# Transposing V in fp32 through a shared ring of PSUM banks in a cross-covariance attention kernel

## The chip, the cores and the metric

The kernel runs on one core of one Trainium2 chip. The metric is the device time of one execution in microseconds (us). Beside the times there is one execution recorded by the hardware profiler, from which all views come.

The engines are named as in the profile: PE is TensorE (matrix multiplies and transposes), PEld its weight loads, DVE is VectorE, ACT is ScalarE, POOL is GpSimd, and SP is SyncE, which issues every transfer of this kernel. SPq is SP's own instruction queue. SBUF is the core's working memory. PSUM is the memory that PE writes its results into; it has eight banks of 2 KB for each of the 128 partitions.

## What is computed

```python
def setup_inputs():
    batch, heads, seq, dim = 8, 12, 512, 64      # Q, K, V: float32
...
    Q_norm = Q / (np.linalg.norm(Q, axis=-2, keepdims=True) + 1e-10)
    K_norm = K / (np.linalg.norm(K, axis=-2, keepdims=True) + 1e-10)
    attn = np.einsum('bhnd,bhne->bhde', Q_norm, K_norm)
    attn = np.exp(attn - np.max(attn, axis=-1, keepdims=True))
    attn = attn / (np.sum(attn, axis=-1, keepdims=True) + 1e-10)
    return np.einsum('bhnd,bhde->bhne', V, attn).astype(np.float32)
```

There are 96 heads. For each, Q and K give a 64 x 64 matrix, which is normalised by the column norms, put through a softmax along its rows, and then multiplied from the left by V. Three inputs and one output of 12.6 MB each make 50.3 MB of transfers.

## The kernel before

Four heads make a unit, and there are 24 units (`U`). One transfer brings Q, K or V of a unit as a tile of 128 partitions x 1024 fp32 (512 KB): each head takes 32 partitions (`NV`), each holding 16 rows (`R`) of 64 values.

Per unit the work is this. `cast_q` and `cast_k` (VectorE) round Q and K into one bf16 tile `qkb`. `grams` (L94) multiplies it by its own transpose, 64 small matmuls, so that one 128 x 128 result per head holds K'Q as well as the squared norms on its diagonal; it goes to `gbuf`, which takes four PSUM banks and exists once. `norms` (L106) takes the diagonals out on VectorE, and GpSimd raises them to the power -1/2 (`rq`, L111). `keep_kq` (L99, ScalarE) copies the K'Q part out of `gbuf`, `scale_k` (L116, GpSimd) scales it, `logits` (L122) transposes it on PE in fp32, `scale_q` (L126) scales it again, `exps` (L130) takes the exponential and `normalise` divides by the row sums. The result is a bf16 matrix in `abuf`; `doubled` (L152) puts a copy of it onto the other 64 partitions, by a matmul and a copy on ScalarE.

V needs a transpose, as its rows must become columns for the last multiply. `cast_v` (L87) rounds it to bf16 into `vb`. `vtrans` (L144) transposes eight 128 x 128 blocks on PE into the bank `vps`, and ScalarE copies the whole bank to SBUF as `vt` (L147), interleaving two blocks on the way. `outs` (L163) multiplies, in two halves of eight matmuls, each half into one bank `po`, and copies each half into `so` (L167). `store` sends `so` out.

PSUM is split so: four banks for `gbuf`, one for the logits and the doubled matrix (`lg` and `dup`), one for `vps`, two for `po`.

The order is written out by hand. The main loop runs over `s`, one step for each unit of Q and K, and is pipelined by hand: step `s` casts unit s + 1, makes the grams and norms of s, the logits of s - 1, and the normalised matrix of s - 2. V and outputs lag behind by the rule `outs_by`, four units in five steps, so that of five steps four have one V and one output. Every engine executes its own instructions in the order written. SP issues the loads three units ahead, and stores three units late, in one queue; at most eight transfers are under way.

When the main loop ends, 16 units have their outputs. The tail does the other eight: `gbuf`'s four banks are freed for transposes (`ps_t`), VectorE takes over the casts of V, and the two copies of an output are split between ScalarE and VectorE (`both`).

Of the kernel before, what the change touches and what calls it, by code (L numbers as in the profile page):

```python
# [8 lines left out]
F32 = mybir.dt.float32  # L9
BF16 = mybir.dt.bfloat16  # L10
# [4 lines left out]
D = 64  # L15
HU = 4
NV = 32
R = 16
SV = 2
MV = 64  # L20
TP = 4
# [3 lines left out]
def kernel(  # L25
# [7 lines left out]
    nc = tc.nc  # L33
    B, H, N, _ = Q.shape
    assert N == NV * R and Q.shape[3] == D
    U = B * H // HU
# [5 lines left out]

    const = ctx.enter_context(tc.tile_pool(name="const", bufs=1))
    qp = ctx.enter_context(tc.tile_pool(name="qp", bufs=5))
    vp = ctx.enter_context(tc.tile_pool(name="vp", bufs=6))
    vbp = ctx.enter_context(tc.tile_pool(name="vbp", bufs=4))
    qkp = ctx.enter_context(tc.tile_pool(name="qkp", bufs=4))
    vtp = ctx.enter_context(tc.tile_pool(name="vtp", bufs=3))
    sop = ctx.enter_context(tc.tile_pool(name="sop", bufs=10))
    small = ctx.enter_context(tc.tile_pool(name="small", bufs=4))  # L50
    main = ctx.enter_context(ExitStack())
    ps_v = ctx.enter_context(tc.tile_pool(name="ps_v", bufs=1, space=bass.MemoryType.PSUM))
    ps_l = ctx.enter_context(tc.tile_pool(name="ps_l", bufs=1, space=bass.MemoryType.PSUM))
    ps_o = ctx.enter_context(tc.tile_pool(name="ps_o", bufs=2, space=bass.MemoryType.PSUM))

    LOAD_AHEAD = 3

    def outs_by(s):

        return max(0, (s - 2) * 4 // 5)  # L60


    qf, kf, vf, vb, qkb, nsq, rq, kqs, sl, ex, vt, so, kq = ({} for _ in range(13))

    def load_qk(u):
        qf[u] = qp.tile([128, R, D], F32, name="qf")
# [4 lines left out]
    def load_v(u):  # L71
        vf[u] = vp.tile([128, R * D], F32, name="vf")
        nc.sync.dma_start(out=vf[u], in_=Vf[u])

    def store(u, g=slice(0, SV)):
        nc.sync.dma_start(out=Of[u][:, g], in_=so[u][:, g].rearrange("p s t d -> p s (t d)"))
# [4 lines left out]

    def cast_k(u):
        nc.vector.tensor_copy(qkb[u][:, :, D:], kf[u])  # L83

    def cast_v(u, copy=nc.scalar.copy):
        w = vb[u] = vbp.tile([128, R // 2, 2 * D], BF16, name="vb")
        copy(w.rearrange("p t d -> p (t d)"), vf[u])  # L87

    def grams(u):

# [29 lines left out]
    def logits(u):  # L120
        for h in range(HU):
            nc.tensor.transpose(lg[:, h, :], kqs[u][D:, h, :], ident[D:, D:])  # L122

    def scale_q(u):
        s = sl[u] = small.tile([D, HU, D], F32, name="sl")
        nc.vector.tensor_tensor(out=s, in0=lg, in1=rq[u][0:D, :, None].to_broadcast([D, HU, D]), op=ALU.mult)  # L126

    def exps(u):
        e = ex[u] = small.tile([D, HU, D], F32, name="ex")
        nc.scalar.activation(e, sl[u], AF.Exp)  # L130

    def normalise(u):
        s = small.tile([D, HU], F32, name="esum")
        nc.vector.reduce_sum(out=s, in_=ex[u], axis=AX.X)  # L134
        ri = small.tile([D, HU], F32, name="rinv")
        nc.vector.reciprocal(ri, s)
        a = abuf[u % len(abuf)]
        nc.vector.tensor_tensor(out=a[0:D, :, 0, :], in0=ex[u], in1=ri[:, :, None].to_broadcast([D, HU, D]), op=ALU.mult)  # L138

    def vtrans(u, pool=ps_v):  # L140

        ps = pool.tile([128, R // 2, 128], BF16, name="vps")
        for t in range(R // 2):
            nc.tensor.transpose(ps[:, t, :], vb[u][:, t, :], identb)  # L144

        w = vt[u] = vtp.tile([128, TP, 128, 2], BF16, name="vt")
        nc.scalar.copy(w.rearrange("p t c a -> p a t c"), ps.rearrange("p (a t) c -> p a t c", a=2))  # L147

    def doubled(u):

        a = abuf[u % len(abuf)]
        nc.tensor.matmul(dup[D:], identb[0:D, 0:D], a[0:D, :, 0, :], tile_position=(0, D))  # L152
        nc.scalar.copy(a[D:, :, 1, :], dup[D:])  # L153

    def outs(u, copies=(nc.scalar.copy, nc.scalar.copy)):
        s = so[u] = sop.tile([128, SV, TP, 2 * D], F32, name="so")
        a = abuf[u % len(abuf)]
        for g in range(SV):
            po = ps_o.tile([128, TP, 2 * D], F32, name="po")
            for t in range(TP):  # L160
                for x in range(2):
                    h = 2 * g + x
                    nc.tensor.matmul(  # L163
                        po[MV * x:MV * (x + 1), t, :], vt[u][:, t, NV * h:NV * (h + 1), :].rearrange("p c a -> p (c a)"),
                        a[:, h].rearrange("p a d -> p (a d)"), tile_position=(0, MV * x),
                    )
            copies[g](s[:, g], po)  # L167

    ps_g = main.enter_context(tc.tile_pool(name="ps_g", bufs=1, space=bass.MemoryType.PSUM))
    gbuf = ps_g.tile([128, HU, 512], F32, name="gram")  # L170
# [8 lines left out]
    ident = const.tile([128, 128], F32, name="ident")  # L179
    make_identity(nc, ident)  # L180
    identb = const.tile([128, 128], BF16, name="identb")
# [4 lines left out]
    for i in range(12):  # L186
        a = const.tile([128, HU, 2, D], BF16, name=f"ab{i}")
# [3 lines left out]
    def on(f, u):  # L191
        if 0 <= u < U:
            f(u)
# [5 lines left out]
    nv, nst, nt = 2, 0, 0  # L199
    for s in range(U):  # L200
        n0, n1 = outs_by(s - 1), outs_by(s)
        on(load_qk, s + LOAD_AHEAD)
        while nv < min(U, n1 + 4):
            load_v(nv)
            nv += 1
        while nst < n1 - 3:
            store(nst)
            nst += 1
        new = range(nt, n1 + 1) if s >= 1 else ()
        for v in new:  # L210
            cast_v(v)
        on(cast_q, s + 1)
        on(normalise, s - 2)
        on(grams, s)
        on(norms, s)
        on(keep_kq, s)
        on(scale_k, s)
        on(logits, s - 1)
        on(scale_q, s - 1)
        on(exps, s - 1)  # L220
        on(cast_k, s + 1)
        for v in range(n0, n1):
            outs(v)
        on(doubled, s - 2)
        for v in new:
            vtrans(v)
            nt = v + 1

    last = U - 1
    main.close()  # L230
    ps_t = ctx.enter_context(tc.tile_pool(name="ps_t", bufs=4, space=bass.MemoryType.PSUM))
    both = (nc.scalar.copy, nc.vector.tensor_copy)

    def v_ahead(u):
        if u + 1 < U:
            vtrans(u + 1, ps_t)

    def cast_ahead(u):
        if u < U:
            cast_v(u, nc.vector.tensor_copy)  # L240

    def move(u):
        on(load_v, u + 4)
        store(u - 3)

    cast_ahead(n1 + 1)
    cast_ahead(n1 + 2)
    for i, u in enumerate(range(n1, U)):
        move(u)
        v_ahead(u)  # L250
        if i == 0:
            normalise(last - 1)
        if i == 1:
            logits(last)
            scale_q(last)
            exps(last)
        if i == 2:
            normalise(last)
        if i >= 1:
            cast_ahead(u + 2)  # L260
        outs(u, both)
        if i == 0:
            doubled(last - 1)
        if i == 2:
            doubled(last)
# [34 lines left out]
```

## Time and profile before

| | |
|---|---|
| median of 3 runs | 134.99 us (133.66 to 135.82) |
| the profiled execution | 131.46 us, span of the core 129.7 us |
| transfers | 50.34 MB in 97 of 512 KB or less, all issued by SP |
| rows of V: cast on ScalarE, L87 | 17, 1046 ns each |
| cast on VectorE, L87 | 7, 679 ns each |
| copy of vt, L147 | 24, 1311 ns each |
| copies of so, L167 | 40 on ScalarE, 593 ns; 8 on VectorE, 688 ns |
| last gram | ends at 108.0 us |
| last copy into so | starts at 125.3 us |

A row of a group in the profile reads: line, engine, operation, result <- inputs with their shapes, how often; then busy time and mean ns of one; then how long the engine sat idle just before these instructions, and on whom it waited. In the view of waits, a row says who waited for whom, the sum in us, the number of times and the longest. "Granted clock" is the share of full speed at which PE runs; in this profile it is either 1.0 or 0.5 at any moment. A clock of 1.0 is also what the view prints ahead of the first record, which comes after some 43 us here; in the first 31 us the 64 gram matmuls take 1.89 us as they do at half clock later, against 1.07 us at full clock.

### The profile page before, as it was taken

How to read it: one execution, taken by the hardware profiler on the slowest of the kernel's cores; microseconds unless marked ns; L12 is line 12 of the kernel's file. 1: busy time of each engine (PE TensorE's matmuls, PEld its weight loads, DVE VectorE, ACT ScalarE, POOL GpSimd, SP SyncE). 2: the span in 40 equal slices, each digit the busy share in tenths (PEclk: the TensorE clock that was granted, in tenths of full speed). 3: DMA queues.
4: the chain of work that ended last, by engine and by line, in shares of the span. 5: the costliest groups of instructions: out<-in, count | busy, mean ns of one | idle time of the engine just before them, and what ended most of it. 6: DMA issues, size and time to landing. Idle time of an engine off the chain costs nothing.

```text
span 129.7 us, 5416 instructions
## 1 busy us (share of the span) xinstructions
PE 90.5 (70%) x2232; PEld 69.5 (54%) x2232; DVE 94.7 (73%) x351; ACT 96.8 (75%) x154; POOL 71.0 (55%) x68
## 2 busy tenths in 40 slices
PE   0034878699677789859866996567999774968630
PEld 0043666568455668638543874455768553745520
DVE  0776687985987788785988498698956968588640
ACT  3002442658999958999995879999779999889960
POOL 7924467773873578383778368187717773500000
PEclk9999999999999555995896579998555999599996
DMA  4999999999999999999999999999999999989885
GB/s 140 394 417 418 412 401 411 408 402 407 409 402 412 412 409 408 414 407 411 407 418 406 416 409 416 410 415 413 410 416 408 409 403 419 407 336 361 324 318 214
DMA packets 16936, 50.67 MB, mean 391 GB/s; under 512 B 1552, under 2 KB 1552, under 8 KB 16912
## 3 DMA queue, kind: packets, MB, share of 16 engines
q1 hardware_dynamic: 16912, 50.34, 97.9%
q8 instruction: 17, 0.28, 0.8%
q14 instruction: 7, 0.06, 0.1%
HBM read 37.75 MB, written 12.58 MB: 388 GB/s over the span
## 4 chain that ended last, share of the span: by engine, by line
ACT 32%; PE 26%; DMA 14%; DVE 9%; POOL 8%; issue 7%; SPq 1%; ACTq 0%; POOLq 0%; DVEq 0%
DMA qf<-in_Q_dram 14%; ACT vt L147 12%; ACT so L167 8%; PE gram L94 8%; PE po L163 7%; PE vps L144 6%; POOL rq L111 6%; ACT vb L87 3%; PE lgdup L122 3%; ACT kq L99 3%; DVE scr L106 3%; ACT ab L153 3%; ACT ex L130 2%; PE lgdup L152 2%; POOL kqs L116 2%
## 5 line engine op out<-in xcount | busy, mean ns | idle before, releaser
L111 POOL TENSOR_TENSOR rq<-nsq,mhalf 128x4 f32<-128x4 f32 x24 | 49.3, 2056 | 38.2 <-DVE nsq L106 23.1
L94 PE MATMUL gram<-qkb 32*128 32x128 bf16 x1536 | 37.3, 264 | 15.5 <-DVE qkb L83 11.6
L94 PEld LDWEIGHTS <-qkb 32*128 32x128 bf16 x1536 | 31.2, 119 | 24.3 <-DVE qkb L83 17.8
L106 DVE CUSTOM_DVE_ANT_0 scr<-gram,ident 128x128 f32<-128x128 f32 x96 | 22.1, 284 | 16.2 <-PE gram L94 16.2
L147 ACT COPY vt<-vps 128x1024 bf16<-128x1024 bf16 x24 | 31.5, 1311 | 1.6 <-PE vps L144 1.0
L99 ACT COPY kq<-gram 64x256 f32<-64x256 f32 x24 | 8.8, 367 | 23.2 <-DVE nsq L106 22.9
L80 DVE CAST qkb<-qf 128x1024 bf16<-128x1024 f32 x24 | 19.3, 803 | 5.0 <-DMA qf<-in_Q_dram 4.9
L167 ACT COPY so<-po 128x512 f32<-128x512 f32 x40 | 22.1, 593 | 0.9 <-PE po L163 0.5
L163 PE MATMUL po<-ab,vt 128*64 128x128 bf16 x384 | 19.2, 251 | 4.6 <-ACT so L167 2.2
L144 PE MATMUL vps<-identb,vb 128*128 128x128 bf16 x192 | 18.2, 250 | 1.5 <-DVE vb L87 1.3
L163 PEld LDWEIGHTS <-vt 128*64 128x64 bf16 x384 | 14.5, 128 | 8.5 <-ACT vt L147 4.6
L87 ACT CAST vb<-vf 128x1024 bf16<-128x1024 f32 x17 | 17.8, 1046 | 0.7 <-DMA vf<-in_V_dram 0.6
L144 PEld LDWEIGHTS <-vb 128*128 128x128 bf16 x192 | 13.2, 111 | 8.2 <-DVE vb L87 3.2
L122 PE MATMUL lgdup<-ident,kqs 64*64 64x64 f32 x96 | 12.6, 269 | 7.1 <-POOL kqs L116 6.6
L116 POOL TENSOR_TENSOR kqs<-kq,rq 64x256 f32<-64x256 f32 x24 | 15.1, 628 | 2.2 <-POOL rq L111 0.4
L83 DVE CAST qkb<-kf 128x1024 bf16<-128x1024 f32 x24 | 16.2, 676 | 0.0
L122 PEld LDWEIGHTS lgdup<-ident,kqs 64*64 64x64 f32 x96 | 7.9, 134 | 11.6 <-POOL kqs L116 9.5
L126 DVE TENSOR_TENSOR sl<-lgdup,rq 64x256 f32<-64x256 f32 x24 | 9.9, 414 | 3.7 <-PE lgdup L122 3.0
L152 PE MATMUL lgdup<-ab,identb 64*64 64x256 bf16 x24 | 7.7, 323 | 6.2 <-DVE sl L126 5.6
L130 ACT ACTIVATE ex<-sl 64x256 f32<-64x256 f32 x24 | 10.0, 417 | 1.1 <-DVE sl L126 0.5
L138 DVE TENSOR_TENSOR ab<-ex,rinv 64x256 bf16<-64x256 f32 x24 | 10.2, 425 | 0.8
L134 DVE TENSOR_REDUCE esum<-ex 64x4 f32<-64x256 f32 x24 | 9.7, 405 | 1.3 <-ACT ex L130 1.3
(16 smaller groups left out, 41.6 us busy)
## 6 DMA issues: line engine op xcount, KB each, us to landing
qf<-in_Q_dram SPq DMA_DIRECT2D x24, 512.0 KB, 10.4
kf<-in_K_dram SPq DMA_DIRECT2D x24, 512.0 KB, 10.4
vf<-in_V_dram SPq DMA_DIRECT2D x24, 512.0 KB, 10.0
out_dram<-so SPq DMA_DIRECT2D x23, 512.0 KB, 10.0
out_dram<-so SPq DMA_DIRECT2D x2, 256.0 KB, 2.5
```

The lines of the kernel that those rows point to most:

```text
L80: nc.vector.tensor_copy(qkb[u][:, :, 0:D], qf[u])
L83: nc.vector.tensor_copy(qkb[u][:, :, D:], kf[u])
L87: copy(w.rearrange("p t d -> p (t d)"), vf[u])
L94: nc.tensor.matmul(gbuf[:, h, 0:2 * D], x, x, start=(t == 0), stop=(t == R - 1), tile_position=(NV * h, 0))
L106: nc.vector.tensor_tensor_reduce(out=scr, in0=gbuf[:, h, 0:2 * D], in1=ident, scale=1.0, scalar=1e-20, op0=ALU.mult, op1=ALU.add, accum_ou ...
L111: nc.gpsimd.tensor_tensor(out=r, in0=n2, in1=mhalf, op=ALU.pow)
L116: nc.gpsimd.tensor_tensor(out=kk[D:], in0=kq[u][D:], in1=rq[u][D:, :, None].to_broadcast([D, HU, D]), op=ALU.mult,)
L122: nc.tensor.transpose(lg[:, h, :], kqs[u][D:, h, :], ident[D:, D:])
L144: nc.tensor.transpose(ps[:, t, :], vb[u][:, t, :], identb)
L147: nc.scalar.copy(w.rearrange("p t c a -> p a t c"), ps.rearrange("p (a t) c -> p a t c", a=2))
L163: nc.tensor.matmul(po[MV * x:MV * (x + 1), t, :], vt[u][:, t, NV * h:NV * (h + 1), :].rearrange("p c a -> p (c a)"), a[:, h].rearrange("p ...
L167: copies[g](s[:, g], po)
```

## The change

The cast of V is dropped, with its buffers. PE transposes V straight from the fp32 tile as it came from memory, so the results are fp32 and a unit needs two banks instead of one: `vtrans` handles half a unit at a time. PE writes each block into every second word of the bank, so that the two blocks are interleaved already, and the copy out of PSUM, which reads and writes in order, rounds to bf16. In the main loop the half transposes and the half outputs share one pool of three banks (named `pv`) and are interleaved in the order: output half 0, `doubled`, transpose half 0, output half 1, transpose half 1. In the tail the half transposes still have four banks of their own, and their copies are split between ScalarE and VectorE. V has eight buffers instead of six. The aim is to take the cast off ScalarE and VectorE.

```diff
-    vp = ctx.enter_context(tc.tile_pool(name="vp", bufs=6))
-    vbp = ctx.enter_context(tc.tile_pool(name="vbp", bufs=4))
+    vp = ctx.enter_context(tc.tile_pool(name="vp", bufs=8))
...
-    ps_v = ctx.enter_context(tc.tile_pool(name="ps_v", bufs=1, space=bass.MemoryType.PSUM))
     ps_l = ctx.enter_context(tc.tile_pool(name="ps_l", bufs=1, space=bass.MemoryType.PSUM))
-    ps_o = ctx.enter_context(tc.tile_pool(name="ps_o", bufs=2, space=bass.MemoryType.PSUM))
+    ps_o = ctx.enter_context(tc.tile_pool(name="ps_o", bufs=3, space=bass.MemoryType.PSUM))
...
-    def cast_v(u, copy=nc.scalar.copy):
-        w = vb[u] = vbp.tile([128, R // 2, 2 * D], BF16, name="vb")
-        copy(w.rearrange("p t d -> p (t d)"), vf[u])
...
-    def vtrans(u, pool=ps_v):
-
-        ps = pool.tile([128, R // 2, 128], BF16, name="vps")
-        for t in range(R // 2):
-            nc.tensor.transpose(ps[:, t, :], vb[u][:, t, :], identb)
-
-        w = vt[u] = vtp.tile([128, TP, 128, 2], BF16, name="vt")
-        nc.scalar.copy(w.rearrange("p t c a -> p a t c"), ps.rearrange("p (a t) c -> p a t c", a=2))
+    def vtrans(u, i, copy=nc.scalar.copy, pool=ps_o):
+
+
+        if i == 0:
+            vt[u] = vtp.tile([128, TP, 128, 2], BF16, name="vt")
+        ps = pool.tile([128, TP // 2, 128, 2], F32, name="pv")
+        for t in range(TP // 2):
+            for a in range(2):
+                c = (a * TP + i * TP // 2 + t) * 2 * D
+                nc.tensor.transpose(ps[:, t, :, a], vf[u][:, c:c + 2 * D], ident)
+        copy(vt[u][:, i * TP // 2:(i + 1) * TP // 2], ps)
...
-    def outs(u, copies=(nc.scalar.copy, nc.scalar.copy)):
-        s = so[u] = sop.tile([128, SV, TP, 2 * D], F32, name="so")
+    def outs(u, g, copy=nc.scalar.copy):
+        if g == 0:
+            so[u] = sop.tile([128, SV, TP, 2 * D], F32, name="so")
         a = abuf[u % len(abuf)]
-        for g in range(SV):
-            po = ps_o.tile([128, TP, 2 * D], F32, name="po")
...
+        po = ps_o.tile([128, TP, 2 * D], F32, name="pv")
...
-        for v in new:
-            cast_v(v)
...
-        for v in range(n0, n1):
-            outs(v)
-        on(doubled, s - 2)
-        for v in new:
-            vtrans(v)
-            nt = v + 1
+        work = [(outs, v, g) for v in range(n0, n1) for g in range(SV)]
+        for i, (v, g) in enumerate((v, g) for v in new for g in range(2)):
+            work.insert(2 * i + 1, (vtrans, v, g))
+        for i, (f, v, g) in enumerate(work):
+            if i == 1:
+                on(doubled, s - 2)
+            f(v, g)
+        if len(work) < 2:
+            on(doubled, s - 2)
+        nt = max(nt, n1 + 1) if s >= 1 else nt
...
-    def move(u):
+    for i, u in enumerate(range(n1, U)):
         on(load_v, u + 4)
         store(u - 3)
-
-    cast_ahead(n1 + 1)
-    cast_ahead(n1 + 2)
-    for i, u in enumerate(range(n1, U)):
-        move(u)
-        v_ahead(u)
+        if u + 1 < U:
+            for g in range(2):
+                vtrans(u + 1, g, both[g], ps_t)
...
-        if i >= 1:
-            cast_ahead(u + 2)
-        outs(u, both)
+        for g in range(SV):
+            outs(u, g, both[g])
```

## The prediction

> **What bounds the kernel now.** I read the page first, then the waits of the DMA queue, the rows of the groups that the diff touches, ScalarE's order of time in one stretch, and a table by stretches.
>
> ```profile
> PE 90.5 (70%) x2232; PEld 69.5 (54%) x2232; DVE 94.7 (73%) x351; ACT 96.8 (75%) x154; POOL 71.0 (55%) x68
> ...
> PEclk9999999999999555995896579998555999599996
> DMA  4999999999999999999999999999999999989885
> GB/s 140 394 417 418 412 401 411 408 402 407 409 402 412 412 409 408 414 407 411 407 418 406 416 409 416 410 415 413 410 416 408 409 403 419 407 336 361 324 318 214
> ...
> q1 hardware_dynamic: 16912, 50.34, 97.9%
> ```
>
> No engine is over 75% busy, but the DMA engines are full from the second slice to the 35th at about 410 GB/s. 50.34 MB at 410 GB/s is 122.8 us of the 129.7 us span. So transfers bound everything up to about 113 us. What an engine saves there is worth nothing by itself. In the last five slices of 3.24 us the rate falls: they sum to 1553 where 2050 would be full, a shortfall of 497 x 3.24 / 410 = 3.9 us.
>
> ```profile
> SPq L73 <- DMA qf<-in_Q_dram: 11.0, 12, 1.4
> SPq L76 <- DVE so L167: 10.3, 7, 2.4
> SPq L69 <- DMA kf<-in_K_dram: 8.4, 9, 1.3
> ```
>
> SyncE, which issues all transfers, mostly waits for older transfers (eight are under way: issues 1.27 us apart, landing 10 us later). The row that differs is L76: seven stores wait 10.3 us for the copy into so. These are the stores of the tail. There computing decides.
>
> ```profile
> 42.00:51.50 9.50, 8.23 (x187) 6.46 (x190) 8.08 (x32) 7.67 (x15) 7.12 (x6) 0.50 1.03 411
> 75.50:90.00 14.50, 9.99 (x339) 7.59 (x336) 12.20 (x49) 13.95 (x24) 10.39 (x8) 0.97 1.03 412
> 116.00:120.00 4.00, 2.98 (x56) 2.04 (x50) 3.53 (x7) 3.88 (x6) 0.00 (x0) 1.00 0.91 351
> 120.00:124.00 4.00, 2.44 (x51) 2.05 (x48) 2.33 (x4) 4.00 (x6) 0.00 (x0) 1.00 0.82 308
> ```
>
> Columns: the stretch, its length, busy PE, weight loads, DVE, ACT, POOL, then granted clock, DMA share, GB/s. At full clock ScalarE is the fullest engine (13.95 of 14.5), at half clock TensorE (8.23 of 9.5); both kinds keep DMA at 1.03. In the tail ScalarE is busy 4.00 of 4.00 and DMA falls to 0.82.
>
> ```profile
> 75.61 0.37 ACT L99 COPY kq<-gram 64x256 f32<-64x256 f32 x1 [0.60 <-DVE nsq L106]
> 76.00 0.42 ACT L130 ACTIVATE ex<-sl 64x256 f32<-64x256 f32 x1
> 76.44 1.07 ACT L167 COPY so<-po 128x512 f32<-128x512 f32 x2
> 77.54 0.37 ACT L153 CAST ab<-lgdup 64x256 bf16<-64x256 f32 x1
> 77.93 1.30 ACT L147 COPY vt<-vps 128x1024 bf16<-128x1024 bf16 x1
> 79.09 1.04 ACT L87 CAST vb<-vf 128x1024 bf16<-128x1024 f32 x1
> 80.16 0.37 ACT L99 COPY kq<-gram 64x256 f32<-64x256 f32 x1
> ```
>
> One step at full clock: ScalarE runs without a gap, 4.55 us from one kq to the next. A step with a V and a store moves four transfers, 4 x 1.27 = 5.1 us; four steps in five are such. So ScalarE is 0.5 us per step under the floor.
>
> **What the Trainium skill says.** "TensorE: Matmul & The Clock Gate", section "Weight-path perf modes", has fast weight load for non-FP32 only; section "LDWEIGHTS" prices a load by its columns at 1.2 GHz: an estimate of 107 ns for 128 fp32 columns. The trace agrees in size: four 64-column fp32 transposes of L122 take 0.41 us at full clock, against 0.24 for one, so 0.057 each and 0.11 for twice the columns; at half clock 0.63 against 0.31, so 0.107 and 0.21. Its section "Terms" also mentions a transpose mode four times faster for fp32; no row of before shows it. "PSUM — Partial Sum Buffer", section "Specifications (TRN2)": transposes write their input type, so fp32 fills a bank with half a unit, and non-contiguous writes slow matmuls. The new transposes write every second word; no row of before does that.
>
> **The change part by part.**
>
> ```profile
> L147 ACT COPY vt<-vps 128x1024 bf16<-128x1024 bf16 x24 | 31.5, 1311 | 1.6 <-PE vps L144 1.0
> L167 ACT COPY so<-po 128x512 f32<-128x512 f32 x40 | 22.1, 593 | 0.9 <-PE po L163 0.5
> L144 PE MATMUL vps<-identb,vb 128*128 128x128 bf16 x192 | 18.2, 250 | 1.5 <-DVE vb L87 1.3
> L87 ACT CAST vb<-vf 128x1024 bf16<-128x1024 f32 x17 | 17.8, 1046 | 0.7 <-DMA vf<-in_V_dram 0.6
> ```
>
> The cast goes: 17 x 1.046 = 17.8 us of ScalarE in the loop and 7 x 0.68 = 4.7 us of VectorE in the tail. The copy of 1.311 us becomes two halves from fp32 PSUM. The nearest row is L167, same elements and source: 0.593 each, 1.19 a unit (bounds 0.56 and 0.66, half of 1.31). A V step of ScalarE is then 0.37 + 0.42 + 1.19 + 0.37 + 1.19 = 3.5 us instead of 4.7. In the loop the full DMA hides this.
>
> The transposes: eight a unit, before (0.62 - 0.22) / 7 = 0.057 apart at full clock and 0.103 at half. I take 0.11 and 0.21 (0.88 and 1.7 us a unit), that is +0.4 and +0.9. Lower bound 0.057, as bf16. Upper bound twice mine, if the strided writes bind.
>
> The added wait: outputs and half transposes now take turns in three banks, in the order out 0, doubled, half 0, out 1, half 1. Half 1 needs out 0's bank, so it waits for ScalarE's copy of out 0, which stands behind kq and ex of this step. Behind half 1 on TensorE stand the next step's grams, and behind these VectorE's norms. The new cycle at full clock: grams 1.2 to the first norm, norms 0.95, sl 0.42, ex 0.44, out 0's copy 0.6, half 1 0.5 = 4.1 us, still under 5.1. At half clock TensorE itself fills it: grams 1.65, four logits 0.43, outs 0.95, doubled 0.2, transposes 1.7, waits 0.5 = 5.4 us, 0.3 over. The steps of 2.5 us transfer with no V make it worse on the average of 4.6, but half-clock phases last some 10 us, alternate with full-clock ones, and end sooner if TensorE stays busier; eight transfers under way bridge them. I cost the loop at 0.
>
> V's load now waits for a transpose rather than a cast; with eight buffers for six, and the queue full of older transfers, nothing. The shorter DVE queue in the tail swaps a cast of 0.68 for half a copy of about 0.69: nothing. That leaves ScalarE in the tail: 1.31 + 0.60 becomes 0.6 + 0.6. The last outputs start 1.66 us apart (121.31, 122.98, 124.64). Then VectorE with 0.69 + 0.69 and TensorE with 0.88 + 0.45 bind, at about 1.4. From 110.8 to 126.0 eight units take 15.2 us; eight at 1.4 and some 1.5 for the last unit's logits and normalising give 12.7, so computing ends 2.5 us sooner. Of the 3.9 us that DMA loses about 1.1 stay, the landing of the last store (2.4 us, of which 1.3 is its data). 2.5 fits into 2.8: gain 2.5.
>
> The times (133.66 to 135.82) lie 2 to 4 us over the profiled execution's 131.46. The data is the same, so I read part of this as computing late under another clock pattern. A lighter ScalarE gives some of it back, 1 us by judgement. 134.99 - 2.5 - 1.0 = 131.5.
>
> **The rivals.** First, slower: TensorE becomes the bound. For it: 8.23 of 9.5 us at half clock, and a longer serial chain. Against: 0.97 clock stretches have TensorE at 10 of 14.5. With 18 V steps 0.6 late, half of them in half clock, it gives 134.99 + 5.4 - 2.5 = 138; all cold, 143; with the upper bound of the transposes over 145.
>
> Second, nothing to see: stores already set the tail's pace. For it: DMA is still 0.91 busy at 351 GB/s from 116 to 120, so a write may be slower than a read, and then an earlier store only queues. Gain 0.5 to 1: about 134.2.
>
> Third, more: the loop was held by ScalarE in the timed executions. With all of the 3.5 us back, 129.
>
> **How the numbers follow.** Forecast (130.3 to 133.3) 0.50; nothing to see 0.22; slower 0.18; more 0.10. 2% lies at 132.3 and 137.7. Of the forecast 0.38 falls under 132.3, with the third case 0.48 faster; of the slower rival 0.16 over 137.7; 0.36 stays within. Range 128.8 to 137.5: from just under the transfers' own limit to the foot of the slower rival.
>
> **What would show it.** Right: no vb, vt copies near 0.6, L147's successor in 48 pieces; DMA at 9 to the end but one or two slices; the tail's wait of stores for so well under 10.3; outputs 1.4 apart. Wrong: DMA slices under 9 before 105 us, grams waiting for half 1 and half 1 for ScalarE; fp32 transposes over 0.2 apart at full clock; or a tail just as long with stores landing later.

## The result, and the profile after

The change makes the kernel slower. Its median is 140.34 us (140.03 to 141.38), against 133.42 us for the kernel before in the same comparison; the ratio is 1.052, with a 95% interval of 1.045 to 1.059. The prediction was 131.5 us with a range that ended at 137.5, so both the size and the direction were wrong. Of its cases the first rival came true (138 us), a little worse than it was worked out. Medians are over all runs of a kernel, and a ratio is taken only from the runs within 1.5% of that kernel's own fastest, so the two can differ where a kernel scatters.

The page of the kernel after, in the parts that were shown of before:

```profile
PE 98.8 (71%) x2232; PEld 73.9 (53%) x2232; DVE 94.1 (68%) x351; ACT 73.4 (53%) x154; POOL 72.1 (52%) x68
...
PEclk9999996558999965999995599999559999999999
DMA  4999999999999999999999999999999877746786
GB/s 153 369 404 418 412 411 408 405 407 406 407 405 417 406 418 407 417 402 412 412 411 410 417 407 419 405 421 407 418 405 372 286 278 225 245 152 228 286 327 227
...
q1 hardware_dynamic: 16912, 50.34, 92.9%
```

ScalarE lost 23 us of work, as it should (96.8 to 73.4). The same bytes were moved. But a slice is 3.46 us here, and in the 31st, which begins at about 104 us, the rate starts to fall (372 GB/s); from the 32nd on the transfers run short: 152 to 327 GB/s where they had 410. The waits of SyncE say for what:

```profile
SPq L74 <- ACT so L164: 14.8, 7, 5.2
SPq L74 <- DVE so L164: 12.1, 7, 3.0
SPq L71 <- DMA qf<-in_Q_dram: 9.7, 11, 1.9
```

Stores (L74) wait 26.9 us for their outputs; before, the same two rows had 2.3 and 10.3. So the outputs come late. By how much, and since when, is seen from three marks in the two orders of time:

| | before | after |
|---|---|---|
| cast of Q of the last unit starts | 101.98 | 109.81 |
| last gram ends | 107.96 | 116.38 |
| first output matmul of the tail | 110.74 | 118.97 |
| last copy into so ends | 126.00 | about 134.1 |
| span | 129.7 | 138.4 |

Nearly all of the loss, 8.4 of 8.7 us, is there when the main loop ends. The tail, from its first output matmul to its last copy, takes 15.3 us before and 15.1 after. (It ran at full clock throughout after; before, 3.4 us of it were at half clock.) While the loop fell behind, the transfers stayed full, as they were filled with loads that run ahead: SyncE issues the last load of Q and K at 91.1 us before and at 91.0 after, when the loop is already 6 us behind. What could not be made up came out behind the loop, when little but stores was left and there was nothing to store.

Where a step of the loop spends its time is in the order of time. A step of the kernel after at full clock, cut to what stands between the scaled logits and the next grams (start, duration, engine, line):

```profile
42.60 0.41 DVE L120 TENSOR_TENSOR sl<-lgdup,rq 64x256 f32<-64x256 f32 x1
...
43.07 0.27 PE L149 MATMUL lgdup<-ab,identb 64*64 64x256 bf16 x1 [0.66 <-DVE sl L120]
...
43.27 0.66 PE L143 MATMUL pv<-ident,vf 128*128 128x128 f32 x4
...
43.61 0.58 ACT L164 COPY so<-pv 128x512 f32<-128x512 f32 x1
43.85 0.41 PE L160 MATMUL pv<-ab,vt 128*64 128x128 bf16 x8
...
44.25 0.66 PE L143 MATMUL pv<-ident,vf 128*128 128x128 f32 x4
...
44.84 1.07 PE L88 MATMUL gram<-qkb 32*128 32x128 bf16 x64
```

`pv` is the shared pool: from `ab,vt` come the halves of an output, from `ident,vf` the half transposes; out 0 stands ahead of these lines. `sl` ends at 43.01. Only then can `doubled` (L149) write, since it shares its bank with what `sl` reads, and behind it in TensorE's queue stand half 0, out 1, half 1 and the grams. TensorE stood idle 0.66 us in front of it. The grams start 1.83 us after `sl`. The bank wait is there too, at the same time: out 0's copy ends at 44.19 and half 1 starts at 44.25. The same stretch of the kernel before at full clock:

```profile
79.21 0.42 DVE L126 TENSOR_TENSOR sl<-lgdup,rq 64x256 f32<-64x256 f32 x1 [0.34 <-PE lgdup L122]
...
79.86 0.29 PE L152 MATMUL lgdup<-ab,identb 64*64 64x256 bf16 x1
...
80.19 0.62 PE L144 MATMUL vps<-identb,vb 128*128 128x128 bf16 x8
...
80.75 0.46 PE L94 MATMUL gram<-qkb 32*128 32x128 bf16 x20
```

There `sl` ends at 79.63 and the grams start 1.12 us later, with only `doubled` and eight bf16 transposes between. At half clock the stretch after is longer still. Here is one whole cycle of TensorE, from logits to logits, all at half clock:

```profile
97.48 0.63 PE L116 MATMUL lgdup<-ident,kqs 64*64 64x64 f32 x4
...
98.05 0.64 PE L160 MATMUL pv<-ab,vt 128*64 128x128 bf16 x8
...
98.44 0.41 DVE L120 TENSOR_TENSOR sl<-lgdup,rq 64x256 f32<-64x256 f32 x1
...
98.91 0.37 PE L149 MATMUL lgdup<-ab,identb 64*64 64x256 bf16 x1 [0.22 <-DMA qf<-in_Q_dram]
...
99.21 1.12 PE L143 MATMUL pv<-ident,vf 128*128 128x128 f32 x4
...
100.25 0.64 PE L160 MATMUL pv<-ab,vt 128*64 128x128 bf16 x8
...
100.82 1.12 PE L143 MATMUL pv<-ident,vf 128*128 128x128 f32 x4
...
101.87 1.89 PE L88 MATMUL gram<-qkb 32*128 32x128 bf16 x64
...
103.70 0.43 PE L116 MATMUL lgdup<-ident,kqs 64*64 64x64 f32 x4
```

The grams start 3.0 us after `sl`, which ends at 98.85. (The idle 0.22 us is put down to a DMA that landed then; what `doubled` needed was `sl`.) It is TensorE's only gap: the cycle takes 6.22 us, and TensorE is full. The kernel before at half clock has 1.5 us between:

```profile
96.45 0.41 DVE L126 TENSOR_TENSOR sl<-lgdup,rq 64x256 f32<-64x256 f32 x1
...
97.05 0.42 PE L152 MATMUL lgdup<-ab,identb 64*64 64x256 bf16 x1
...
97.40 1.03 PE L144 MATMUL vps<-identb,vb 128*128 128x128 bf16 x8
...
98.36 1.78 PE L94 MATMUL gram<-qkb 32*128 32x128 bf16 x64
```

Now the length of a step, from one unit's first gram to the next unit's. Taken are steps with a V that lie wholly at one clock, without the step ahead of one that has no V (4.6 us before, 4.9 after). At full clock it is 4.2 us after and 3.9 to 4.1 before, at half clock 6.4 after (one step) and 5.0 to 5.2 before. So most of the loss is made at half clock. The order of time agrees: the kernel after falls behind in four jumps of 1.9 to 3.3 us, each around one of its stretches at half clock (21.9 to 32.1, 49.2 to 56.0, 73.1 to 79.9 and 97.0 to 103.8 us), and between them the distance changes by less than 1 us. (The kernel before has its half-clock stretches at other times, so a single jump is not a clean measure. Its first one ends well before 43 us: its grams at 29.33 take 1.89 us, those at 33.34 take 1.07.)

Two things are new between `sl` and the grams: what stands there (out 1 and the transposes in two pieces, by the order of the work and by the three banks), and what a transpose costs in fp32. The experiments take them apart.

### The profile page after: what moved, and what is told of

Its sections match the earlier page's. It is cut to its first block, busy times and chain, and to the rows that moved or that the text cites. A ratio compares the mean times of both kernels' runs of the same rounds, so it can differ in the third digit from the quotient of the medians.

```text
span 138.4 us, 5433 instructions
## 1 busy us (share of the span) xinstructions
PE 98.8 (71%) x2232; PEld 73.9 (53%) x2232; DVE 94.1 (68%) x351; ACT 73.4 (53%) x154; POOL 72.1 (52%) x68
## 4 chain that ended last, share of the span: by engine, by line
DMA 42%; PE 33%; DVE 15%; issue 3%; POOL 2%; SPq 1%; DVEq 0%; POOLq 0%
DMA qf<-in_Q_dram 27%; PE pv L143 15%; DMA vf<-in_V_dram 15%; PE gram L88 10%; DVE scr L100 6%; PE pv L160 5%; PE lgdup L149 3%; DVE sl L120 2%; POOL rq L105 2%; DVE vt L144 2%; DVE ab L132 1%; DVE qkb L78 1%; DVE qkb L81 1%; DVE nsq L100 1%; DVE esum L128 1%
## 5 line engine op out<-in xcount | busy, mean ns | idle before, releaser
L88 PE MATMUL gram<-qkb 32*128 32x128 bf16 x1536 | 33.5, 246 | 14.5 <-DVE qkb L81 11.8
L88 PEld LDWEIGHTS <-qkb 32*128 32x128 bf16 x1536 | 27.8, 109 | 25.5 <-DVE qkb L81 18.6
L93 ACT COPY kq<-gram 64x256 f32<-64x256 f32 x24 | 8.8, 367 | 49.7 <-DVE nsq L100 47.5
L143 PE MATMUL pv<-ident,vf 128*128 128x128 f32 x192 | 34.3, 315 | 0.3 <-ACT so L164 0.3
L143 PEld LDWEIGHTS pv<-ident,vf 128*128 128x128 f32 x192 | 23.4, 157 | 17.6 <-PE pv L160 11.3
L144 ACT CAST vt<-pv 128x512 bf16<-128x512 f32 x41 | 24.2, 591 | 3.8 <-PE pv L143 3.3
L164 ACT COPY so<-pv 128x512 f32<-128x512 f32 x40 | 23.5, 587 | 1.4 <-PE pv L160 0.5
L160 PE MATMUL pv<-ab,vt 128*64 128x128 bf16 x384 | 20.2, 239 | 0.2 <-DVE vt L144 0.2
L149 PE MATMUL lgdup<-ab,identb 64*64 64x256 bf16 x24 | 6.9, 289 | 17.2 <-DVE sl L120 14.4
L160 PEld LDWEIGHTS <-vt 128*64 128x64 bf16 x384 | 13.1, 117 | 6.5 <-issue 5.0
L116 PE MATMUL lgdup<-ident,kqs 64*64 64x64 f32 x96 | 11.3, 246 | 2.4 <-POOL kqs L110 2.4
L150 ACT CAST ab<-lgdup 64x256 bf16<-64x256 f32 x24 | 8.8, 367 | 2.8 <-PE lgdup L149 2.2
```

The costliest lines, as they stand in the source:

```text
L88: nc.tensor.matmul(gbuf[:, h, 0:2 * D], x, x, start=(t == 0), stop=(t == R - 1), tile_position=(NV * h, 0))
L143: nc.tensor.transpose(ps[:, t, :, a], vf[u][:, c:c + 2 * D], ident)
L144: copy(vt[u][:, i * TP // 2:(i + 1) * TP // 2], ps)
L160: nc.tensor.matmul(po[MV * x:MV * (x + 1), t, :], vt[u][:, t, NV * h:NV * (h + 1), :].rearrange("p c a -> p (c a)"), a[:, h].rearrange("p ...
L164: copy(so[u][:, g], po)
```

## The experiments

Each was timed beside the kernel before, whose median was 133.49 us for the first four and 133.92 or 133.93 us for the others.

**Doubled last.**

```diff
-            if i == 1:
-                on(doubled, s - 2)
             f(v, g)
-        if len(work) < 2:
-            on(doubled, s - 2)
+        on(doubled, s - 2)
```

> Edit: the changed kernel with `doubled` moved from the second place of a step's work to the last. Theories. Order: after sl, TensorE still has doubled, half 0, out 1 and half 1 before the next grams (1.7 us at full clock, 3.0 at half), because doubled waits for sl and all stands behind it. Then half 0 and out 1 slip ahead of sl; at half clock that saves about 1.2 us a step, at full clock little, as half 1 still waits for out 0's copy. 136 to 138 us. Bank: only the wait of half 1 for its bank counts; 140 us, unchanged. Price: only what the fp32 transposes cost on TensorE counts; 140 us, unchanged.

Measured: 139.74 us (139.33 to 140.35), ratio 1.055 (1.045 to 1.065). Almost nothing came back; the order theory had asked for 136 to 138. The waits show why:

```profile
PEld pv L143 <- ACT so L164: 12.8, 13, 1.4
PE gram L88 <- DVE qkb L81: 11.8, 7, 8.4
PE pv L143 <- ACT so L164: 10.7, 13, 1.2
```

With `doubled` out of the way, half 1 stands waiting for its bank, 10.7 us in 13 steps. After the change itself that row had 0.3 us: there the two obstacles lay over each other and the profile named only the first. At full clock the grams now start 2.0 us after `sl`.

**Out 0 early.**

```diff
         on(grams, s)
+        work = [(outs, v, g) for v in range(n0, n1) for g in range(SV)]
...
+        first = work[:1] if n1 > n0 else []
+        for f, v, g in first:
+            f(v, g)
         on(norms, s)
...
+        on(doubled, s - 2)
+        for f, v, g in work[len(first):]:
             f(v, g)
```

> Edit: the changed kernel with out 0 put right behind the grams, so that its copy comes ahead of kq and ex on ScalarE and half 1 finds its bank free; doubled stays ahead of half 0. Order: half 0, out 1 and half 1 still stand behind doubled and sl, some 1.6 us at full clock; 138.5 to 140 us. Bank: the loop is as short as before, 132 to 134 us. Price: 140 us.

Measured: 141.74 to 151.06 us in four runs, median 146.79; the runs scatter too much for a ratio. It is no faster than the change, where the bank theory had asked for 132 to 134 and the order theory for no more than 140. No row of half 1 waiting for `so` is left, so the bank wait is gone, and still the loop is late. The bank wait alone is thus not the cause. TensorE's wait for `sl` in front of `doubled`, 14.4 us after the change, is here:

```profile
PE lgdup L149 <- DVE sl L120: 18.7, 22, 3.4
```

The stretch behind `sl` is as long as ever, 1.8 us at full and 3.0 at half clock. How much slower than the change this order is stays open: the profiled run took 147.25 us and was at half clock for 24 us towards the end of its loop.

**Both.** Out 0 behind the grams, `doubled` last.

> Edit: both at once, out 0 behind the grams and doubled last. Order: nothing of the transposes is left behind sl at full clock; the cycle is then TensorE's own work at half clock, 4.9 us, and 3.8 at full; 131.5 to 134 us, with the gain more than the sum of the two alone. Bank: as with out 0 early alone, 132 to 134. Price: 139 to 140 us.

Measured: 134.73 us (131.24 to 137.85) in twenty runs, ratio 1.001 (0.993 to 1.008) from the fastest four. By the ratio the loss is gone; by the medians 1.2 us of some 7 are left. This is with the same fp32 transposes and the same three banks. Neither move alone gave it, so the two obstacles are in parallel: each is enough to hold the grams back. In the profiled run (136.08 us) the last gram ends at 110.1, against 116.4 after the change and 108.0 before, so 6.3 of the 8.4 us in the loop are back; its tail, at half clock from 112.1 to 119.0, takes 16.8 us. A step of this kernel at full clock:

```profile
55.66 0.41 DVE L120 TENSOR_TENSOR sl<-lgdup,rq 64x256 f32<-64x256 f32 x1
...
55.96 0.41 PE L160 MATMUL pv<-ab,vt 128*64 128x128 bf16 x8
...
56.30 0.66 PE L143 MATMUL pv<-ident,vf 128*128 128x128 f32 x4
...
56.89 0.29 PE L149 MATMUL lgdup<-ab,identb 64*64 64x256 bf16 x1
57.11 1.07 PE L88 MATMUL gram<-qkb 32*128 32x128 bf16 x64
```

`sl` ends at 56.07, when half 0 is done and out 1 under way, and the grams start 1.04 us later instead of 1.83.

**The price of fp32.** The order and the banks of the change are kept; the transposes read the upper half of each fp32 word as bf16.

```diff
-        ps = pool.tile([128, TP // 2, 128, 2], F32, name="pv")
+        ps = pool.tile([128, TP // 2, 2, 128], BF16, name="pv")
+        raw = vf[u].bitcast(BF16).rearrange("p (f w) -> p f w", w=2)[:, :, 1]
...
-                nc.tensor.transpose(ps[:, t, :, a], vf[u][:, c:c + 2 * D], ident)
+                nc.tensor.transpose(ps[:, t, a, :], raw[:, c:c + 2 * D], identb)
-        copy(vt[u][:, i * TP // 2:(i + 1) * TP // 2], ps)
+        copy(vt[u][:, i * TP // 2:(i + 1) * TP // 2], ps.rearrange("p t a c -> p t c a"))
```

> Edit: the changed kernel, order and banks kept, with the upper half words of V's fp32 read as bf16 by the transposes (V is cut off rather than rounded to bf16), written in order, and interleaved by the copy as before. A transpose should be back at 0.057 us apart at full clock. Price: 131 to 133 us. Order: the chain behind sl shrinks by 0.6 us at full and 1.2 at half clock, the bank wait stays; 134.5 to 137 us. Bank: 139 to 140 us.

Measured: 134.66 us (131.15 to 136.73) in twenty runs, ratio 0.997 (0.991 to 1.004) from the fastest five. By the ratio it lies between the price and the order theory, by the median within the order theory. Taking the fp32 price away gives most or all of the loss back too, without touching the order. The two rows of the transposes, after the change and here:

```profile
L143 PE MATMUL pv<-ident,vf 128*128 128x128 f32 x192 | 34.3, 315 | 0.3 <-ACT so L164 0.3
```

```profile
L144 PE MATMUL pv<-identb,vf 128*128 128x128 bf16 x192 | 20.8, 248 | 2.6 <-ACT so L165 2.4
```

The bank wait now shows as 2.4 us, against none to speak of: it is there, but short. The profiled run (134.83 us) had 17 us of half clock towards the end of its loop, and its last gram still ends 5.3 us later than before; its tail, at full clock, is 2.8 us shorter (12.5 us).

The two remedies act at different clocks. The traces side by side, in us, for the same kind of steps as above (a single figure may be one step only):

| | `sl` to grams, full clock | half clock | grams to grams, full clock | half clock |
|---|---|---|---|---|
| before | 0.8 to 1.1 | 1.5 to 2.1 | 3.9 to 4.1 | 5.0 to 5.2 |
| the change | 1.8 | 3.0 to 3.1 | 4.2 | 6.4 |
| doubled last | 2.0 | 3.0 | 4.4 | 6.3 |
| out 0 early | 1.8 | 3.0 | 4.2 to 4.4 | 6.6 |
| both | 0.7 to 1.1 | 2.3 to 2.4 | 3.4 to 3.9 | 6.0 |
| price of fp32 taken away | 1.55 | 2.0 | 3.9 | 5.2 to 5.4 |

(Single steps stand out from their row. In the first column they are 2.1 after the change, 2.4 with doubled last, 2.0 with both and 1.85 with the price away. In the third they are three late steps of 4.2 to 4.7 with both, and one of 4.7 with the price away.) With bf16 transposes a half-clock step is nearly as short as before. With the order mended it stays at 6.0, as TensorE is full there (busy 6.50 of the 6.50 us from 47.5 to 54.0); but a full-clock step becomes shorter than before, and the loop catches up. So the loss has two conditions: transposes that cost too much at half clock, and an order that leaves no room at full clock to make it up. Lessening either gives most of it back.

**The pool alone.** The kernel before, with its whole bf16 transposes moved into one pool of three banks with the outputs.

```diff
-    ps_v = ctx.enter_context(tc.tile_pool(name="ps_v", bufs=1, space=bass.MemoryType.PSUM))
-    ps_o = ctx.enter_context(tc.tile_pool(name="ps_o", bufs=2, space=bass.MemoryType.PSUM))
+    ps_o = ctx.enter_context(tc.tile_pool(name="ps_o", bufs=3, space=bass.MemoryType.PSUM))
...
-    def vtrans(u, pool=ps_v):
-        ps = pool.tile([128, R // 2, 128], BF16, name="vps")
+    def vtrans(u, pool=ps_o):
+        ps = pool.tile([128, R // 2, 128], BF16, name="po")
```

> Edit: the kernel before, with the whole bf16 transposes and the two halves of an output in one pool of three banks. Three pieces a step in three banks: no piece waits for a copy of its own step. Order: as before, 133 to 134 us. If the shared pool by itself costs (any wait for a bank behind ScalarE's queue): 135 us or more.

Measured: 133.43 us, ratio 1.000 (0.997 to 1.003). Sharing costs nothing here, where a step has no more pieces than there are banks, and no transpose waits for a copy of `so`. With a fourth piece, which the fp32 results need, such a wait appears: 10.7 us with doubled last, 2.4 with the price taken away.

**The relief alone.** The kernel before, without its cast, by the same reading of upper halves, and with eight buffers of V.

```diff
-        w = vb[u] = vbp.tile([128, R // 2, 2 * D], BF16, name="vb")
-        copy(w.rearrange("p t d -> p (t d)"), vf[u])
+        vb[u] = vf[u].bitcast(BF16).rearrange("p (t d w) -> p t d w", d=2 * D, w=2)[:, :, :, 1]
```

> Edit: the kernel before, its order and banks kept, without the cast of V: the transposes read the upper half words of the fp32 tile as bf16 (V is cut off rather than rounded), with eight buffers of V. It takes 17.8 us off ScalarE and 4.7 us off VectorE at no price on TensorE. If the relief is worth something by itself: 131 us or less. If the transfers hide it in the loop and only the tail gains: 132 to 133 us. If the outputs' tail is not bound by these engines: 133.5.

Measured: 131.61 us (131.28 to 131.92), ratio 0.986 (0.980 to 0.992). So the gain that the change aimed at exists, 2.3 us between the medians, between the two expectations. Its last copy into `so` on ScalarE ends at 124.2, and the transfers of the tail are fuller than those shown of before (0.91 and 0.82 in the same two stretches):

```profile
116.00:120.00 4.00, 2.73 (x56) 2.19 (x57) 1.38 (x2) 3.98 (x6) 0.00 (x0) 1.00 0.94 362
120.00:124.00 4.00, 2.25 (x56) 1.87 (x50) 1.59 (x3) 3.50 (x5) 0.00 (x0) 1.00 0.96 368
```

**Order and price together**, and then with more outputs in the loop (`(s - 2) * 9 // 10` for `(s - 2) * 4 // 5` in `outs_by`).

> Edit: the changed kernel with out 0 behind the grams, doubled last, and bf16 transposes of the upper half words. If the order and the price each only shorten the same chain down to what another cycle allows: 133 to 134.5, as each alone gave. If the loop still had room: 130 to 132 us.

Measured: 133.14 us (132.12 to 136.41), ratio 0.996 (0.992 to 1.000). By the ratios nothing to speak of is added to what either gave alone; by the medians it is 0.8 us under before, where each alone was 1.2 above. Both figures lie in what was expected if the two shorten the same chain.

> Edit: as the run before it, with nine outputs in ten steps rather than four in five, so that 18 outputs and not 16 are done in the loop and the tail has six units. If what is lost is that too many outputs are left when the loop ends, and transfers run dry there: 129 to 131.5 us. If the loop cannot take more: 133 to 136 us.

Measured: 133.16 us (131.28 to 134.18) in four runs. It decides nothing between the two.

> Edit: the kernel before without the cast (upper half words transposed as bf16, V cut off rather than rounded), and nine outputs in ten steps rather than four in five. If the outputs left for the tail are what keeps it from the transfers' limit: 129.5 to 131 us, under the 131.6 of the same kernel at four in five. If more work in the loop makes the loop late instead: 132 to 134 us.

Measured: 131.57 us (131.07 to 131.68) against 133.92, ratio 0.983 (0.980 to 0.985). It beats both kernels, but it is no better than the same kernel at four in five by their medians (131.61), so the share of outputs in the loop isn't shown to matter.

> Edit: the changed kernel, fp32 transposes kept, with out 0 behind the grams, doubled last, and nine outputs in ten steps. Order: with the chain behind sl gone the loop takes it, and the tail of six units at 1.6 us each ends sooner: 131.5 to 134 us. If TensorE is then full at half clock: 135 to 138 us.

Measured: 131.16 to 139.58 us in nine runs, median 134.42, ratio 0.980 (0.975 to 0.986) from the fastest two. Its median is above that of before; the scatter leaves open whether it is a gain.

## Why the prediction was wrong, point by point

**What bounds the kernel.** The reading that the transfers are full up to 113 us and that the tail waits for `so` was right. The conclusion drawn from it, that computing in the loop has slack, was not. The change shows that the loop can fall 8 us behind while DMA stays at 9 in every slice but the first up to the 31st. The waits of the kernel before held a sign of it:

```profile
DVE qkb L80 <- DMA qf<-in_Q_dram: 4.9, 2, 4.1
```

VectorE waits for a load of Q only twice, both times before 21 us, and never for one of K. So the 5.1 us that a step's four transfers take were no floor under the step (3.9 to 4.1 us at full clock): computing was not paced by the loads, and what a step gains in length moves all that follows. Full transfers showed that loads were ahead. They did not show that outputs could be late for nothing.

**The loop at 0.** This is the step that failed. It had two terms. At full clock the prediction worked out a cycle of 4.1 us; measured are 4.2 (grams at 106.90, 111.11 and 115.31). At half clock it summed TensorE's work to 5.4 us; the cycle shown above takes 6.22. Every piece but the waits was sized too low, counted from its start to the start of the next: transposes 2.09 for 1.7, outputs 1.21 for 0.95, grams 1.83 for 1.65, logits 0.57 for 0.43, doubled 0.30 for 0.2, against waits of 0.22 for 0.5. And it then set the excess, 0.3 us by its own sum, to nothing, as bridged by eight transfers under way. A delay in a half-clock step is not bridged, since the loop did not wait for loads. It adds up, to 8.4 us at the end of the loop. (Of the five half-clock phases of before between 42 and 114 us, two last some 10 us, as was assumed, and three last 3.4 to 6.8.) The prediction had listed what is queued behind half 1, but had not seen that `doubled`, in second place, holds half 0 and out 1 behind `sl` as well; with the bank wait beside it, that is why a step at full clock has no room to catch up. The first rival, TensorE as the bound at half clock, had the right mechanism. That its 138 us lie near the 140.34 is partly luck: it took 5.4 us for the loop and a gain of 2.5 in the tail, where 8.4 and 0.1 came, from a median of before that was 1.6 us higher than in the comparison.

**The price of a transpose** was right: eight take 1.09 us at full clock, of which one is 0.273, so 0.117 apart (0.11 predicted); at half clock four take 1.12 with one at 0.477, so 0.21 apart (0.21). The upper bound, for writes to every second word, is not seen: 0.117 is about twice the 0.057 of the dense 64-column transposes. What was missed is that a piece of four at half clock takes 1.04 us from its start to the start of the next piece, not four times 0.21.

**The bank wait** was seen, with the right place in the queue, and counted in the 4.1 us, which came out. Alone it isn't the cause, as out 0 early shows; but with `doubled` moved it is what remains, 10.7 us in 13 steps.

**The copies** were right: 0.591 us for a half on ScalarE (0.593 predicted).

**The tail.** Predicted 12.7 us from the first output matmul to the last copy; measured 15.1. TensorE is its bound, at 1.59 us a unit:

```profile
127.66 1.09 PE L143 MATMUL pv<-ident,vf 128*128 128x128 f32 x8
128.68 0.64 PE L160 MATMUL pv<-ab,vt 128*64 128x128 bf16 x16
129.25 1.09 PE L143 MATMUL pv<-ident,vf 128*128 128x128 f32 x8
130.27 0.64 PE L160 MATMUL pv<-ab,vt 128*64 128x128 bf16 x16
```

Starts are 1.02 and 0.57 apart, where 0.88 and 0.45 were added up from spacings alone. In the first units `doubled` waits for the last two normalisings as well, which stand behind VectorE's new copy (1.26 and 1.19 us idle; before, 0.4 in all). With bf16 transposes the tail took 12.5 us, so the fp32 price is most of what kept the change from its gain here.

**The gain** on the other side was right in direction and too large. The relief by itself brought 2.3 us by medians, where 2.5 for the tail and 1 for the loop had been put. Where it arises isn't shown: the profiled runs of the two kernels (131.28 and 131.46 us) differ by too little.

## What to carry to other kernels

Ask of each piece of work not only how long it takes and whether its engine has room, but what it stands behind and what stands behind it in the queue: cheap room on TensorE in front of a wait is not room behind it. Full transfers in a loop of loads that run ahead do not mean that computing may be late, since a delay of a step adds up unseen and is paid when only stores are left. Look for waits of the engines on loads: where there are none, transfers don't pace the loop. Where two obstacles overlap, removing one shows nothing, so try both at once before you rule either out.

## What the runs showed of the hardware

bf16 transposes whose weights are every second half word of an fp32 tile load as fast as dense ones: 98 ns in the median of 192 weight loads, the same as from the cast tile, against 141 for fp32. That reads fp32 as bf16 with no cast on any engine, if cutting off instead of rounding is good enough. The fp32 transpose follows the granted clock (0.117 us apart at full, 0.21 at half). Its writes to every second word of a bank showed no cost of their own: 0.117 is about twice the 0.057 of the 64-column fp32 transposes, which write in order; the same transpose with writes in order was not run.
